# Input projection of a hybrid encoder layer: second half in reverse token order, low weight parts kept in DRAM

## The chip, the cores and the metric

The kernel runs on one core of a Trainium2 chip. The metric is the device time of one execution in microseconds (us). Three executions of the kernel before took 3480.42, 3481.12 and 3474.23 us (median 3480.42); a further one was recorded by the hardware profiler.

## The reference, cut to what matters

One encoder layer runs on two requests (256 and 2048 tokens, 2304 together, width 1024). Its input projection multiplies the normed and modulated tokens by one matrix whose 3072 columns feed two mixers:

```python
h = rmsnorm(x, norm1_g) * (1 + sc1) + sh1
proj = h @ w_in
hy = hyena_mixer(proj[..., :3 * HY_WIDTH], ...)      # 1536 columns
at = dilated_attention(proj[..., 3 * HY_WIDTH:])     # 1536 columns
mix = jnp.concatenate([rmsnorm(hy, hy_out_g), rmsnorm(at, attn_out_g)], axis=-1) @ w_out
```

Behind it come the output projection, a gated MLP and a last norm. All of it is float32.

## The kernel before, in words

**Products in three matmuls.** A float32 operand is split into a high part (a cast to the fp32r type on ACT, the Scalar engine) and a low part, the rest (a subtraction, `sub` at L203, mostly on DVE, the Vector engine). `mm3` (L208 to L210) adds high x high, weight-high x token-low and weight-low x token-high in one PSUM bank.

**Projection.** `project` works on three token passes of 768 own tokens (`PASS`, `OWN`) and, within a pass, on twelve tiles `m` of 128 columns. It is called twice: for the hyena columns (tiles 0 to 11, woven with the generation of the long filters, `filters`) and for the attention columns (tiles 12 to 23, woven with the hyena convolution and the remaining adaLN vectors, `ada_vector`). For each tile `load_w` loads 512 KB of weights (`wiraw`, L580), makes `wihi` on ACT (L583) and `wilo` on DVE (L203, called from L584), each from a pool of two buffers; then 48 matmuls per tile go to `pj`, ACT copies them out to `u` (L627, L629), and the result is transposed to token rows (`pjt`, `tt`) or stored (`d_qT`, `d_kT`). The hyena tiles also pass a short convolution (`cv`, POOL L656, DVE L659 and L662); POOL is the GpSimd engine.

**Input of a pass.** `modulated` loads eight tiles `x` (L489), multiplies them by the inverse norm (`normed`, DVE L519) and modulates them (ACT L553); `split` then makes `hThi` (ACT L571) and `hTlo` (DVE L203). The pool holds one set of the split input, so each pass's split replaces the last one's. The program names the loads of the next pass at tile `ms[5]`; the `x` tiles have eight buffers.

**Filters.** `filters` makes `F` on DVE (L439) from matmuls `fw` (L432, L433), splits it (`fhi` on ACT, `flo` on POOL), multiplies (`fs`), copies out (`fae`, ACT L420) and stores (`d_fA`, L421).

**Order.** The generators are woven by the rates in `RATES`; a scheduler of the framework then sets each engine's order of instructions, and may put one well ahead of its place in the program. SP (SyncE) issues nearly all DMAs, in one queue in order: a DMA that waits holds back those behind it.

Of the kernel before, what the change touches and what calls it, by code (L numbers as in the profile page):

```python
# [13 lines left out]
F32 = mybir.dt.float32  # L14
# [7 lines left out]
P = 128  # L22
# [167 lines left out]
class Hybrid:  # L190
# [331 lines left out]
    def first_input(self, wp, w2, psp):  # L522

        nc = self.nc
        X = []
        for i, (c0, n) in enumerate(self.PASS[0]):
            acc = w2.tile([P, 2, self.RW], F32, tag="rsacc", name="rsacc", bufs=1)[:, :, :n]
            for j in range(0, 8, 2):
                x = self.x_tile(wp, c0, n, j)
                X.append((i, j, c0, n, x))  # L530
                if j == 0:
# [5 lines left out]
            self.x_rstd(psp, acc, c0, n)  # L537
            for _, _, _, _, x in X[4 * i:]:
                self.normed(x, c0, n)
        return X  # L540

    def modulate(self, X, both=False):

        nc = self.nc
        for i, j, c0, n, x in X:
            for k in range(2):
                for r, s, e in self.segs(c0, n):
                    xs = x[:, k, s:e]
                    ga, sh = self.ga[:, 0, j + k, r:r + 1], self.mod[:, 0, j + k, r:r + 1]
                    if both and k:  # L550
                        nc.vector.tensor_scalar(out=xs, in0=xs, scalar1=ga, scalar2=sh, op0=ALU.mult, op1=ALU.add)
                    else:
                        nc.scalar.activation(xs, xs, AF.Identity, scale=ga, bias=sh)  # L553
        return X
# [19 lines left out]

    XB = 8

    def load_w(self, wp, src, k, tag, n=8, raws=3, bufs=2):
        nc = self.nc
        raw = wp.tile([P, 8, P], F32, tag="wraw", name=tag + "raw", bufs=raws)[:, :n]
        nc.sync.dma_start(out=raw, in_=src)  # L580
        hi = wp.tile([P, 8, P], F32R, tag="whi", name=tag + "hi", bufs=bufs)[:, :n]
        lo = wp.tile([P, 8, P], F32R, tag="wlo", name=tag + "lo", bufs=bufs)[:, :n]
        nc.scalar.copy(hi, raw)  # L583
        self.sub(nc.vector, lo, raw, hi)  # L584
        return hi, lo

    def project(self, hp, wp, w2, psp, ms, H=None):

        nc, a = self.nc, self.a
        pending = []  # L590

        def flush():
            while pending:
                pending.pop(0)()

        def to_tokens(src, dst, o0, o1, k):
            def go():
                for t0 in range(0, 6, 3):
                    ps = psp.tile([P, 512], F32, tag="pt", name="pjt", bufs=2)
                    for t in range(3):  # L600
                        nc.tensor.transpose(ps[:, t * P:(t + 1) * P], src[:, (t0 + t) * P:(t0 + t + 1) * P],
                                            self.ident)
                    if t0 == 0:
                        tt = wp.tile([P, 6, P], F32, tag="tt", name="tt", bufs=2)
                    nc.vector.tensor_copy(tt[:, t0:t0 + 3], ps[:, :3 * P].rearrange("p (t c) -> p t c", c=P))
                nc.sync.dma_start(out=dst[o0:o1].rearrange("(t p) c -> p t c", p=P)[:, :, k * P:(k + 1) * P], in_=tt)
            return go

        for p in range(3):
            if p == 0 and H is None:  # L610
                X = self.modulated(wp, 0)
            if p or H is None:
                H = [[], []]
                self.split(hp, X, H)
            yield
            o0, o1 = self.OWN[p]
            base = self.PASS[p][0][0]
            for m in ms:
                wh, wl = self.load_w(wp, a["w_in"][m], m, "wi", raws=2)
                u = wp.tile([P, 772], F32, tag="u", name="u", bufs=2)  # L620
                for (c0, n), hs in zip(self.PASS[p], H):
                    ps = psp.tile([P, 512], F32, tag="ps", name="pj")
                    for j in range(8):
                        self.mm3(ps[:, :n], wh[:, j], wl[:, j], hs[j][0], hs[j][1], j == 0, j == 7)
                    us = u[:, c0 - base:c0 - base + n]
                    if 12 <= m < 16:
                        nc.scalar.mul(us, ps[:, :n], -0.125)  # L627
                    else:
                        nc.scalar.copy(us, ps[:, :n])  # L629
                flush()  # L630
                src = u[:, o0 - base:o1 - base]
                if m < 12:
                    src = self.short_conv(w2, u, base, o0, o1, m)
                k = m % 4
                if 12 <= m < 20:
                    dst = self.qT if m < 16 else self.kT
                    nc.sync.dma_start(out=dst[k * P:(k + 1) * P, o0:o1], in_=src)
                else:
                    dst = self.tok[("hv", "x1", "x2", "", "", "av")[m // 4]]
                    pending.append(to_tokens(src, dst, o0, o1, k))  # L640
                yield
                if p < 2 and m == ms[2] and w2 is not None:
                    yield from self.input_rstd(wp, w2, psp, p + 1)
                if p < 2 and m == ms[5]:
                    X = self.modulated(wp, p + 1)
        flush()

    def short_conv(self, wp, u, base, o0, o1, m):
# [395 lines left out]
    def mixers(self):  # L1044
        R = self.RATES
        proj, first, atn, left, hy = (ExitStack() for _ in range(5))
        ps = self.pool(proj, "p_ps", bufs=2, space=PSUM, side="right")
        psF = self.pool(left, "f_ps", bufs=2, space=PSUM, side="left")
        hp = self.pool(proj, "p_h", side="right")
        wp = self.pool(proj, "p_w", side="right")  # L1050
        w2 = self.pool(first, "p_w2", side="right")
        self.rs = hp.tile([P, NT], F32, name="rs")
        f = self.filters(psF)
        with ExitStack() as st:
            ap = self.pool(st, "ada1", side="right")
            rows = self.ada_rows(ap)
            X = self.first_input(wp, w2, ps)
            self.weave([[self.ada_tensor(ap, psF), 8, 0], [self.ada_vector(0, ap, rows, 3, range(4, 8)), 4, 0]])
            self.ada_finish(0)
        H = [[], []]  # L1060
        for i in range(0, 8, 4):
            self.split(hp, self.modulate(X[i:i + 4], True), H)
        g = self.project(hp, wp, w2, ps, range(0, 12), H)
        for x in (g, f, f, f):
            next(x)
        self.weave([[f, R["f"], 0], [g, R["p1"], 0]])
        left.close()
        first.close()
        hb = self.pool(hy, "h_c", side="left")
        self.hyena_consts(hb)  # L1070
        wh = self.pool(hy, "h_w", side="left")
        psH = self.pool(hy, "h_ps", bufs=3, space=PSUM, side="left")

        def units():
            for r in range(2):
                yield from self.hyena(wh, psH, r)

        h = [units(), R["h1"], 0]
        with ExitStack() as st:
            ap = self.pool(st, "ada2", side="left")  # L1080

            def rest():
                rows = self.ada_rows(ap)
                for i in (2, 3, 4, 5):
                    yield from self.ada_vector(i, ap, rows, 1)
                    self.ada_finish(i)

            g = self.project(hp, wp, None, ps, range(12, 24))
            rs = rest()
            gw = [g, R["p2"], 0]  # L1090
            self.weave([h, [rs, R["ad"], 0], gw], until=rs)
        mq = ExitStack()
        self.qkp = self.pool(mq, "m_q", side="left")
        first = self.qk_tiles(self.qkp, 3)
        gw[0] = islice(g, 35 - gw[2])
        self.weave([h, gw], until=gw[0])
        gw[0] = g
        x = self.prepare(0, first)
        self.weave([h, gw, [x, 5, 0]], until=g)
        self.pre = x  # L1100
        proj.close()
        psS = self.pool(atn, "m_psS", bufs=2, space=PSUM, side="right")
        psT = self.pool(atn, "m_psT", bufs=2, space=PSUM, side="right")
        psO = self.pool(atn, "m_psO", bufs=1, space=PSUM, side="right")
        ow = ExitStack()
        self.ow = self.pool(ow, "m_r", side="right")
        h[1:] = [R["h2"], 0]
        self.weave([[self.attention(self.pool(atn, "m_a", side="right"), psS, psT, psO, first, mq), R["at"], 0], h])
        atn.close()
        return hy, mq, ow  # L1110
# [576 lines left out]
```

## Time and profile before

| | us |
|---|---|
| median of three executions | 3480.42 |
| the profiled execution | 3475.7 |
| its span, first to last instruction | 3473.9 |
| TensorE (PE) busy in the span | 3256.6 |
| DVE busy in the span | 2459.5 |

The page of the profile gives per engine the busy time and its share of the span, and cuts the span into 40 slices of 86.8 us with a busy digit in tenths. PEclk is the granted TensorE clock in tenths of full speed. In the trace the first matmul of the projection starts at 51.2 us and the last at 984.0 us; tiles 0 to 11 of the last hyena pass end shortly before 543 us, where the first attention tile's result is copied out. The first matmul of the attention itself starts at 994.8 us.

### The profile page before, as it was taken

To read this page: it belongs to the slowest core of one execution; us is meant where nothing else is said; L and a number is where in the kernel's file an instruction comes from. 1 tells how busy PE (TensorE), PEld (TensorE's weight loads), DVE (VectorE), ACT (ScalarE), POOL (GpSimd) and SP (SyncE) were. 2 spreads that over 40 slices of the span, in tenths; PEclk is the share of its full clock that TensorE was granted. 3 is DMA by queue.
4 is the path that set the end of the run, shared out by engine and by line. 5 is a ranking of instruction groups with operands and counts; after the bars stand their busy time and mean duration, and the time that the engine had idled before them with its cause. 6 is when DMAs were issued, how large, how long until landed. Compare 5 with 4: busy or idle time off the path is not lost.

```text
span 3473.9 us, 56909 instructions
## 1 busy us (share of the span) xinstructions
PE 3256.6 (94%) x20926; PEld 3001.6 (86%) x20926; DVE 2459.5 (71%) x4233; ACT 1559.7 (45%) x2895; POOL 1279.4 (37%) x1018
## 2 busy tenths in 40 slices
PE   7988899989989998998898899999999999899998
PEld 4877788778867786777898899999999999899998
DVE  7988878777576667744886766776866667457657
ACT  4576753233245645455554433334433334344443
POOL 1487661133233423210544433334533335123222
PEclk9999999999999999999899999999999999999999
DMA  6454457777585867584676523445443224557555
GB/s 246 133 163 136 149 173 234 229 255 231 192 227 176 246 189 214 173 257 137 181 214 201 186 97 123 151 163 206 148 159 143 97 90 148 181 181 239 201 192 172
DMA packets 408910, 628.02 MB, mean 181 GB/s; under 512 B 29007, under 2 KB 232015, under 8 KB 402711
## 3 DMA queue, kind: packets, MB, share of 16 engines
q1 hardware_dynamic: 355472, 593.13, 52.6%
q10 hardware_dynamic: 52072, 28.40, 2.8%
q8 instruction: 166, 2.72, 0.3%
q0 software_dynamic: 1088, 2.85, 0.2%
q14 instruction: 112, 0.92, 0.1%
HBM read 419.03 MB, written 205.25 MB: 180 GB/s over the span
## 4 chain that ended last, share of the span: by engine, by line
PE 42%; DVE 5%; DMA 2%; issue 2%; ACT 1%; POOL 1%; SPq 0%; ACTq 0%; DVEq 0%; POOLq 0%
PE w L210 9%; PE w L208 9%; PE w L209 9%; PE fd L210 5%; PE fd L209 5%; PE fd L208 5%; DVE fT L1252 1%; DMA hl<-d_opT 0%; DMA d_x1T<-ox 0%; DVE ohy L1160 0%; DVE ox L1215 0%; PE om L208 0%; POOL oat L1146 0%; PE om L209 0%; PE om L210 0%
## 5 line engine op out<-in xcount | busy, mean ns | idle before, releaser
L208 PE MATMUL w<-hh,whi 128*128 128x288 f32 (+1 forms) x2464 | 735.6, 299 | 13.2 <-ACT whi L1346 8.4
L210 PE MATMUL w<-hh,wlo 128*128 128x290 f32 (+1 forms) x2464 | 733.5, 299 | 11.2 <-POOL wlo L203 7.0
L209 PE MATMUL w<-hl,whi 128*128 128x288 f32 (+1 forms) x2464 | 735.4, 299 | 2.7 <-DVE hl L203 2.7
L208 PEld LDWEIGHTS w<-hh,whi 128*128 128x128 f32 x2464 | 471.1, 191 | 14.5 <-ACT whi L1346 8.6
L210 PEld LDWEIGHTS w<-hh,wlo 128*128 128x128 f32 x2464 | 470.4, 191 | 13.2 <-POOL wlo L203 8.0
L209 PEld LDWEIGHTS w<-hl,whi 128*128 128x128 f32 x2464 | 472.7, 192 | 3.4 <-DVE hl L203 3.2
L208 PE MATMUL pj<-hThi,wihi 128*128 128x386 f32 (+1 forms) x1152 | 402.4, 350 | 12.9 <-ACT u L629 5.4
L209 PE MATMUL pj<-hTlo,wihi 128*128 128x386 f32 (+1 forms) x1152 | 399.3, 347 | 7.1 <-DVE hTlo L203 7.1
L210 PE MATMUL pj<-hThi,wilo 128*128 128x386 f32 (+1 forms) x1152 | 401.7, 349 | 0.0
L208 PE MATMUL fd<-hh,dwh 128*128 128x288 f32 x1210 | 360.3, 298 | 12.6 <-ACT dwh L1552 12.6
L210 PE MATMUL fd<-hh,dwl 128*128 128x288 f32 x1210 | 359.0, 297 | 0.0
L209 PE MATMUL fd<-hl,dwh 128*128 128x288 f32 x1210 | 357.9, 296 | 0.0
L208 PEld LDWEIGHTS pj<-hThi,wihi 128*128 128x128 f32 x1152 | 220.2, 191 | 28.3 <-issue 7.8
L208 PEld LDWEIGHTS fd<-hh,dwh 128*128 128x128 f32 x1210 | 230.0, 190 | 13.2 <-ACT dwh L1552 12.8
L209 PEld LDWEIGHTS pj<-hTlo,wihi 128*128 128x128 f32 x1152 | 220.6, 192 | 23.9 <-issue 9.7
L210 PEld LDWEIGHTS pj<-hThi,wilo 128*128 128x128 f32 x1152 | 219.9, 191 | 11.7 <-issue 7.5
L209 PEld LDWEIGHTS fd<-hl,dwh 128*128 128x128 f32 x1210 | 229.6, 190 | 0.4
L210 PEld LDWEIGHTS fd<-hh,dwl 128*128 128x128 f32 x1210 | 228.0, 188 | 0.1
L939 PEld LDWEIGHTS aOp<-aV,aPT 128*128 128x128 f32 x1408 | 184.3, 198 | 48.8 <-issue 18.4
L735 POOL TENSOR_TENSOR ht<-ht,ht 128x512 f32<-128x512 f32 x72 | 101.7, 1413 | 338.4 <-DVE ht L734 268.2
L203 POOL TENSOR_TENSOR wlo<-ws,whi 128x512 fp32r<-128x512 f32 x88 | 131.6, 1495 | 232.3 <-ACT whi L1346 225.4
L203 POOL TENSOR_TENSOR hl<-hl,hh 128x576 fp32r<-128x576 f32 (+1 forms) x66 | 116.1, 1766 | 264.6 <-ACT hh L1494 191.4
(298 smaller groups left out, 7950.1 us busy)
## 6 DMA issues: line engine op xcount, KB each, us to landing
hl<-d_G SPq DMA_DIRECT2D x154, 288.0 KB, 5.1
dwl<-d_S SPq DMA_DIRECT2D x59, 704.0 KB, 4.9
wiraw<-in_w_in SPq DMA_DIRECT2D x72, 512.0 KB, 4.6
d_G<-cv SPq DMA_DIRECT2D x42, 576.0 KB, 2.9
wraw<-in_w_gate SPq DMA_DIRECT2D x22, 1024.0 KB, 4.8
wraw<-in_w_up SPq DMA_DIRECT2D x22, 1024.0 KB, 4.9
adat<-in_ada_t SPq DMA_DIRECT2D x36, 512.0 KB, 5.6
d_fA<-fae SPq DMA_DIRECT2D x72, 256.0 KB, 2.5
```

What stands on the lines that cost most here:

```text
L203: eng.tensor_tensor(out=lo, in0=x, in1=hi.bitcast(F32), op=ALU.subtract)
L208: mm(out, wh, xh, start=first, stop=False, skip_group_check=more)
L209: mm(out, wh, xl, start=False, stop=False, skip_group_check=more)
L210: mm(out, wl, xh, start=False, stop=last, skip_group_check=more)
L735: nc.gpsimd.tensor_tensor(out=t1, in0=t1, in1=t2, op=ALU.add)
L939: nc.tensor.matmul(po[:, i, hs], pe[:, hh, c], vt[:, x["v"] + c * x["vs"], hs], start=(c == 0), stop=(c == n - 1))
L1252: v.tensor_tensor(out=o, in0=x, in1=y, op=ALU.subtract)
```

## The change

`project` takes the order of its passes. The hyena columns keep the order 0, 1, 2. The attention columns go 2, 1, 0, and the first of these passes uses the split input that the hyena columns left (`self.H`), so that it is neither loaded, normed, modulated nor split again. In the hyena columns' first pass each `wilo` is also stored to a DRAM tensor (`d_wlo`, twelve times 512 KB, L590 of the changed kernel); in passes 1 and 2 it is loaded from there (L586) instead of being subtracted on DVE. `wihi` is made as before.

```diff
-    def load_w(self, wp, src, k, tag, n=8, raws=3, bufs=2):
+    def load_w(self, wp, src, k, tag, n=8, raws=3, bufs=2, kept=None, known=False):
...
         nc.scalar.copy(hi, raw)
-        self.sub(nc.vector, lo, raw, hi)
+        if known:
+            nc.sync.dma_start(out=lo.bitcast(F32), in_=kept)
+        else:
+            self.sub(nc.vector, lo, raw, hi)
+            if kept is not None:
+                nc.sync.dma_start(out=kept, in_=lo.bitcast(F32))
         return hi, lo
...
-        for p in range(3):
-            if p == 0 and H is None:
-                X = self.modulated(wp, 0)
-            if p or H is None:
+        lows = self.dr.tile([len(ms), P, 8, P], F32, name=f"d_wlo{ms[0]}") if w2 is not None else None
+        for p, after in zip(passes, passes[1:] + (None,)):
+            if p != passes[0]:
                 H = [[], []]
                 self.split(hp, X, H)
+            self.H = H
...
-                wh, wl = self.load_w(wp, a["w_in"][m], m, "wi", raws=2)
+                wh, wl = self.load_w(wp, a["w_in"][m], m, "wi", raws=2, kept=None if lows is None else lows[m - ms[0]],
+                                     known=lows is not None and p != passes[0])
...
-                if p < 2 and m == ms[2] and w2 is not None:
-                    yield from self.input_rstd(wp, w2, psp, p + 1)
-                if p < 2 and m == ms[5]:
-                    X = self.modulated(wp, p + 1)
+                if after is not None and m == ms[2] and w2 is not None:
+                    yield from self.input_rstd(wp, w2, psp, after)
+                if after is not None and m == ms[5]:
+                    X = self.modulated(wp, after)
...
-        g = self.project(hp, wp, w2, ps, range(0, 12), H)
+        g = self.project(hp, wp, w2, ps, range(0, 12), H, (0, 1, 2))
...
-            g = self.project(hp, wp, None, ps, range(12, 24))
+            g = self.project(hp, wp, None, ps, range(12, 24), self.H, (2, 1, 0))
```

**First place: SP's queue where hyena pass 0 ends and pass 1 begins.** `d_fA<-fae` stores a filter piece, `d_x<-tt` token rows, `x` is the next input, `wiraw` a weight tile. Before:

```order
L580 DMA wiraw<-in_w_in 128x1024
L606 DMA d_x_84<-tt 128x6x128
L421 DMA d_fA_320<-fae 128x512
L489 DMA x<-in_xT 128x2x383
L421 DMA d_fA_320<-fae 128x512
L489 DMA x<-in_xT 128x2x383 x5
L421 DMA d_fA_320<-fae 128x512
L606 DMA d_x_84<-tt 128x6x128
L489 DMA x<-in_xT 128x2x383 x2
L489 DMA x<-in_xT 128x2x386
L580 DMA wiraw<-in_w_in 128x1024
```

The same place in the changed kernel:

```order
L586 DMA wilo<-d_wlo_318 128x1024
L581 DMA wiraw<-in_w_in 128x1024
L421 DMA d_fA_321<-fae 128x512
L612 DMA d_x_84<-tt 128x6x128
L421 DMA d_fA_321<-fae 128x512
L489 DMA x<-in_xT 128x2x383 x2
L421 DMA d_fA_321<-fae 128x512
L489 DMA x<-in_xT 128x2x383 x3
L586 DMA wilo<-d_wlo_318 128x1024
L489 DMA x<-in_xT 128x2x383
L421 DMA d_fA_321<-fae 128x512
L612 DMA d_x_84<-tt 128x6x128
```

A load of `wilo` now stands ahead of nearly every load of `wiraw`, with filter stores and input loads queued behind it.

**Second place: DVE in hyena pass 2.** `F` is a filter piece, `tt` a copy of transposed rows. Before:

```order
L439 TENSOR_TENSOR F_3311<-fw_3317,fE 64x512
L439 TENSOR_TENSOR F_3312<-fw_3317,fE 64x512
L439 TENSOR_TENSOR F_3314<-fw_3324,fE 64x512
L605 COPY tt<-pjt 128x384 x2
L203 TENSOR_TENSOR wilo<-wiraw,wihi 128x1024
L439 TENSOR_TENSOR F_3313<-fw_3324,fE 64x512
L439 TENSOR_TENSOR F_3313<-fw_3406,fE 64x512
```

And now:

```order
L439 TENSOR_TENSOR F_3324<-fw_3330,fE 64x512
L439 TENSOR_TENSOR F_3325<-fw_3330,fE 64x512
L666 SCALAR_TENSOR_TENSOR cv<-u,c_short,cv 128x768
L669 SCALAR_TENSOR_TENSOR cv<-u,c_short,cv 128x767
L439 TENSOR_TENSOR F_3327<-fw_3337,fE 64x512
L439 TENSOR_TENSOR F_3326<-fw_3337,fE 64x512
```

The subtraction that stood between two filter pieces is gone, and the convolution of the tile has moved among them.

**Third place: DVE where the attention columns begin.** `hS` and `hae` belong to the hyena convolution, `adaj` to `ada_vector`. Before:

```order
L203 TENSOR_TENSOR hTlo<-x,hThi 128x772
L203 TENSOR_TENSOR hTlo<-x,hThi 128x2x384
L519 TENSOR_TENSOR x<-x,rs 128x772
L203 TENSOR_TENSOR hTlo<-x,hThi 128x2x384 x2
L687 CAST hS<-hz 64x512 x2
L694 COPY hae<-hs_5147 128x512
L203 TENSOR_TENSOR wilo<-wiraw,wihi 128x1024
L519 TENSOR_TENSOR x<-x,rs 128x772
L605 COPY tt<-pjt 128x384 x2
L203 TENSOR_TENSOR hTlo<-x,hThi 128x2x384
L519 TENSOR_TENSOR x<-x,rs 128x772
L659 SCALAR_TENSOR_TENSOR cv<-u,c_short,cv 128x768
```

And now:

```order
L611 COPY tt<-pjt 128x384 x2
L694 CAST hS<-hz 64x512 x2
L701 COPY hae<-hs_5160 128x512
L666 SCALAR_TENSOR_TENSOR cv<-u,c_short,cv 128x768
L669 SCALAR_TENSOR_TENSOR cv<-u,c_short,cv 128x767
L307 ISA adaj,mod<-adat,crows 128x1024
L307 ISA mod 128x1
L307 ISA adaj,mod<-adat,crows 128x1024
L307 ISA mod 128x1
L611 COPY tt<-pjt 128x384 x2
L203 TENSOR_TENSOR wilo<-wiraw,wihi 128x1024
```

The split of the next input (`hTlo`) and the norming of the one after it (`x<-x,rs`) no longer stand here; the norming of the next pass's input keeps its place beside hyena pass 2, and one later set of loads and normings stands at the next change of pass. From the output projection on, the order of every engine is unchanged.

## Rows read from the trace of the kernel before

**Rows 1.** The page: busy time per engine, and slices of the span.
```profile
PE 3256.6 (94%) x20926; PEld 3001.6 (86%) x20926; DVE 2459.5 (71%) x4233; ACT 1559.7 (45%) x2895; POOL 1279.4 (37%) x1018
...
PE   7988899989989998998898899999999999899998
...
DVE  7988878777576667744886766776866667457657
```

**Rows 2.** Windows: from:to, length, busy us and instructions per engine, clock, DMA share, GB/s.
```profile
core 0: us, PE busy (x) PEld busy (x) DVE busy (x) ACT busy (x) POOL busy (x), PEclk, DMA share, GB/s
205.00:510.00 305.00, 277.40 (x1417) 247.19 (x1418) 258.02 (x261) 207.37 (x362) 228.81 (x150) 0.97 0.48 148
...
570.00:985.00 415.00, 388.68 (x1915) 333.23 (x1915) 281.87 (x391) 114.91 (x183) 104.58 (x67) 0.99 0.67 217
```

**Rows 3.** PE's waits in 205 to 510: total us, times, longest.
```profile
PE fw L432 <- DVE F L439: 13.6, 10, 3.1
PE pj L209 <- DVE hTlo L203: 6.2, 4, 2.1
PE pjt L601 <- DVE cv L662: 3.7, 3, 2.6
PE fs L209 <- POOL flo L203: 3.0, 6, 1.0
```

**Rows 4.** PE's waits in 570 to 985, the two longest.
```profile
PE hs L692 <- POOL hS L203: 12.5, 15, 1.9
PE hs L778 <- DMA hD<-d_hB: 5.5, 2, 4.1
```

**Rows 5.** The `wilo` subtractions alone: all 72 (min/median/max ns), and DVE in 182 to 522, 205 to 510.
```profile
L203 DVE TENSOR_TENSOR wilo<-wiraw,wihi x72: 1201/1226/2848, 31.1 to 958.2; 128x1024 fp32r<-128x1024 f32 x72
...
182.00:522.00 340.00, 38.95 (x24) 0.97 0.51 158
205.00:510.00 305.00, 35.12 (x21) 0.97 0.48 148
```

**Rows 6.** Where the attention columns begin: PE's wait in 510 to 570, and windows.
```profile
PE pj L208 <- ACT u L627: 3.4, 1, 3.4
...
510.00:570.00 60.00, 56.58 (x313) 55.28 (x312) 52.93 (x67) 31.75 (x46) 13.82 (x8) 0.94 0.88 283
...
550.00:570.00 20.00, 16.58 (x79) 15.70 (x78) 16.59 (x23) 11.47 (x19) 0.00 (x0) 0.83 0.82 272
```

**Rows 7.** Groups of 510 to 570: busy us, mean ns | idle before.
```profile
L519 DVE TENSOR_TENSOR x<-x,rs 128x772 f32<-128x772 f32 x8 | 8.5, 1087 | 0.0
L203 DVE TENSOR_TENSOR hTlo<-x,hThi 128x772 fp32r<-128x772 f32 (+1 forms) x8 | 8.0, 1027 | 0.0
...
L553 ACT ACTIVATE x<-x,mod,ga 128x386 f32<-128x386 f32 x16 | 10.3, 701 | 8.4 <-DVE x L519 8.4
L571 ACT CAST hThi<-x 128x772 fp32r<-128x772 f32 (+1 forms) x8 | 6.6, 837 | 1.2 <-PE pj L210 1.1
```

**Rows 8.** Timeline of DVE, first and last norming of the attention columns' first loaded input.
```profile
391.05 2.06 DVE L519 TENSOR_TENSOR x<-x,rs 128x772 f32<-128x772 f32 x1
...
411.90 0.96 DVE L519 TENSOR_TENSOR x<-x,rs 128x768 f32<-128x768 f32 x1
```

**Rows 9.** DMA issues in 205 to 510, then `wiraw` in 510 to 570: KB each, us to landing.
```profile
wiraw<-in_w_in SPq DMA_DIRECT2D x21, 512.0 KB, 4.2
...
wiraw<-in_w_in SPq DMA_DIRECT2D x6, 512.0 KB, 7.4
```

**Rows 10.** Waits of SP's queue in 205 to 510: total us, times, longest.
```profile
SPq L580 <- DVE wilo L203: 50.2, 19, 6.3
SPq L464 <- DVE frn L463: 24.6, 4, 9.8
```

**Rows 11.** Timeline of SP near the end of the projection: start us, us, DMA.
```profile
899.14 1.73 SPq L867 DMA_DIRECT2D Ks<-d_kT  x3
```

**Rows 12.** DVE's longest wait in 205 to 510.
```profile
DVE F L439 <- POOL flo L203: 16.5, 12, 2.0
```

More of the change, by code (lines that the diff above doesn't have):

```diff
@@ L583, in load_w, with project @@
         nc.scalar.copy(hi, raw)
-        self.sub(nc.vector, lo, raw, hi)
+        if known:
[4 more added lines that the diff above has]
+                nc.sync.dma_start(out=kept, in_=lo.bitcast(F32))
         return hi, lo
-    def project(self, hp, wp, w2, psp, ms, H=None):
+    def project(self, hp, wp, w2, psp, ms, H, passes):
         nc, a = self.nc, self.a
```

## The prediction

> **What bounds the kernel now.** I read the page first: TensorE is busy 94% of the span, and the change leaves its matmuls as they are [rows 1]. So a gain can only come out of PE's idle time and out of stretches at a low granted clock, and the digits show where: in the first slices PE stands at 8 and 9 with DVE at 8 and 9 beside it. Next came windows by stage [rows 2]. In 205 to 510 us, hyena passes 1 and 2, PE is busy 277.40 of 305 us, so 27.6 us are idle, and the granted clock is 0.97, so about 0.03 x 305 = 9.2 us more go to stretches at the lower level (1.2 GHz). DVE is busy 258.02 us there, 84.6%. Then I asked what PE waited for in that stretch [rows 3]: DVE ended 13.6 + 6.2 + 3.7 = 23.5 us of it, mostly as filter pieces `F` that came late behind other work in DVE's queue; POOL ended 3.0. In the stage after it (570 to 985) DVE is busy 281.87 of 415 us, 67.9%, and none of PE's longest waits is for DVE; they are for POOL and DMAs [rows 4]. The reader is to see that DVE is what holds PE in the hyena passes, and hardly later.
>
> **Term 1, the subtractions of passes 1 and 2.** 24 subtractions go; they stand between 182 and 522 us and took 38.95 us, 1.62 us each, 21 of them (35.1 us) within 205 to 510 [rows 5]. They are not on PE's path themselves: they fill DVE's queue ahead of `F`, `hTlo` and `cv`. How much wait goes is estimated by a line through two stages: DVE waits cost PE 23.5 / 305 = 7.7% at 84.6% DVE load and nothing at 67.9%. Less 35.1 us, DVE would work 222.9 us in about 293, 76%; the line gives 3.7%, 10.9 us, so 12.6 us saved. The shortest of the 72 subtractions took 1.20 us and the longest 2.85 [rows 5], so part of the 1.62 is waiting, which a neighbour may inherit; at 1.20 us for 21, 25 us go, the load is 79%, the line leaves 15 us, and 8.5 are saved. I take **-11**, between the two, nearer the measured mean. Bounds: 0 (the waits stay, behind POOL) and -23.5.
>
> The Trainium skill ("SBUF — State Buffer", "Who interferes with whom") says that a DVE instruction with two SBUF inputs contends with a GpSimd instruction that reads SBUF, and that the later one blocks fully until the first ends. The spread from 1.20 to 2.85 us of one form agrees with it [rows 5]. By that rule the wait of a removed subtraction passes to the next two-input instruction, and this term would be the lower -8.5.
>
> **Term 2, the clock.** Of the 9.2 us lost at the lower level I let the same share return as of the waits, 11 / 23.5: **-4**. Bounds 0 and -9.2.
>
> **Term 3, the kept input.** One set goes: eight loads of `x`, eight normings (8.5 us of DVE), 16 modulations (10.3 us of ACT), eight casts (6.6 us of ACT) and eight subtractions (8.0 us of DVE) [rows 7]. Which place gets emptier is told by the order: an input is still normed beside hyena pass 2, as at 391 to 412 us before [rows 8] (it is now the attention columns' second pass's), so the work that vanishes is the split and the norming at 530 to 565 us. There PE waited 3.4 us for ACT's copy of `u`, and from 550 to 570 the clock was 0.83, 3.4 us lost [rows 6]. With ACT and DVE free both should go; I take **-6** of 6.8. Bounds 0 and -6.8. The DMAs have it easier too: the share was 0.88 there.
>
> **Term 4, the new loads.** A `wilo` load waits until PE ends the tile two before, because its buffer is one of two; its first use is one tile later. 24 tiles stand in 340 us, 14.2 us each. The nearest row, `wiraw` of equal size, lands after 4.2 us in this stretch and after 7.4 where the DMA share is 0.88 [rows 9]. The new loads within 205 to 510 add 21 x 0.52 MB, 36 GB/s to 148, so the share rises from 0.48 to about 0.60: 4.2 us is nearest, and some 10 us of cover are left. Behind a waiting `wilo` load stand filter stores, `wiraw` and `x` loads, but SP already stands still there: 19 times, 50.2 us in all, its `wiraw` load waited for DVE's `wilo` [rows 10], and that wait goes. Its longest wait on another DVE result is 9.8 us; such a wait ahead of a load gives 14.0 us with landing, just the cover. I take **+1** for a late load at a change of pass. Bounds: 0 and, worked out below, +36.
>
> **Edits at nothing.** The twelve stores of pass 0 wait for a subtraction that the `wiraw` load behind them waited for before, and cover by the tile's own matmuls lets them land; without that cover the next subtraction into the buffer comes one landing (4.2 us) later, still inside a tile. The reversed order makes the first quarter of q and k the last written. But k for the first heads was fetched at 899 us before [rows 11] and the first attention matmul came at 994.8, so some 95 us of projection and convolution hide it; with that gone, attention would start up to 95 us late. The new order of instructions up to the attention's end I cost at 0, unsigned: no row tells a direction.
>
> **Sum:** -11 - 4 - 6 + 1 = **-20**. The profiled execution took 3475.7 us (span 3473.9 and 1.8 around it) and would take 3455.7. It lies 4.7 us below the median of the runs, so against that median the forecast is 3480.4 - 20 = **3460.4 us**.
>
> **Rivals.** (a) *POOL becomes what holds the filters.* POOL is busy 228.81 of 305 us [rows 2], and DVE's longest wait for work is for POOL's `flo`, 16.5 us [rows 12]. If the filter chain runs at POOL's pace, DVE's free time turns into more such waits, and PE's waits for `F` stay. Only term 3 is left: 3474. For it speaks that 16.5; against it that POOL still has 25% free and that much of its busy time is shared waiting.
> (b) *The low parts come late; slower.* In place of a subtraction on a near engine stands a wait for PE's tile end, SP's queue and 512 KB of DMA. It decides once hold and landing exceed a tile's 14.2 us: 9.8 us of hold with 7.4 of landing make 17.2, 3 us too late. With half of the 24 tiles late by that, PE loses 36 us; less 20 gained, +16: 3496. Against it speaks that no row in this stretch shows `wiraw` landing above a median of 4.2, and that 9.8 us of hold came four times only.
> (c) *Full relief.* All waits for DVE and the clock losses of the stretch and of the change of pass go: -23.5 - 9.2 - 6.8 = -39.5, 3441. It needs DVE never to queue, which eight `hTlo` in a row at two changes of pass deny.
> (d) *The change does less than it says:* the kept input only moves the work, since the next pass's is normed beside hyena pass 2 as before. Then term 3 is 0 and the time is 3466. The order speaks against it: one set is gone for good.
>
> **How the numbers follow.** A measurement of this kernel can tell about 0.2%, 7 us, from no change. The forecast (gain between 8 and 32 us) gets 0.57, (d) 0.05, (c) 0.04; all three are faster: 0.66. (a) gets 0.20, read as no change. (b), and a new order that costs later stages more than the gain, get 0.14. The range goes from full relief, 3441, to a little above no change, 3482; that leaves out most of (b) and a small rest below.
>
> **What would show it.** Right: 48 `wilo` subtractions instead of 72; in the hyena passes 1 and 2 (some 15 us shorter) DVE at 75 to 79% and PE's waits for DVE at 8 to 15 us; no wait of PE for a `wilo` load over 1 us; no wait for `u` where the attention columns begin, and a clock of 1.00 there; 985 to the end as long as before within 5 us. Wrong: waits for `wilo<-d_wlo` on PE (b); DVE's wait for `flo` well above 16.5 us with `F` as late as ever (a); or a gain given back in the attention, where the order is new too.

## The result, and the profile after

Four executions of the changed kernel took 3439.68 to 3445.95 us, median **3441.85**; the ratio to the kernel before is 0.9898, 95% interval 0.9881 to 0.9915. Run again later (`e15_again`, below) it gave 0.9902, 0.9884 to 0.9919. Some 70 executions of the kernel before lay beside the experiments, with medians from 3475.1 to 3477.5; taken as 3476, the change gains 34 to 36 us. Forecast was a gain of 20: the direction holds, the range (3441 to 3482) holds by less than 1 us, the size doesn't.

The new profile's span is 3444.2 us, against 3473.9. Here is the window of the hyena passes 1 and 2 in the kernel before, from ACT's last copy of tile 11 to that of tile 35 (columns as in [rows 2]):

```profile
199.80:538.30 338.50, 308.20 (x1595) 277.16 (x1596) 287.85 (x299) 227.44 (x389) 241.18 (x158) 0.97 0.52 161
```

PE's waits in it (total us, times, longest):

```profile
PE fw L432 <- DVE F L439: 16.0, 11, 3.1
PE pj L209 <- DVE hTlo L203: 6.2, 4, 2.1
PE pjt L601 <- DVE cv L662: 4.3, 4, 2.6
PE fs L209 <- POOL flo L203: 3.0, 6, 1.0
```

The same window of the changed kernel:

```profile
202.10:516.00 313.90, 299.71 (x1595) 275.88 (x1594) 255.61 (x275) 219.14 (x374) 230.90 (x161) 0.98 0.66 211
```

And its PE's waits there:

```profile
PE fw L432 <- DVE F L439: 7.1, 5, 2.6
PE pjt L607 <- DVE cv L669: 4.3, 4, 2.1
PE pj L209 <- DVE hTlo L203: 2.3, 2, 1.5
PE fs L209 <- POOL flo L203: 0.5, 1, 0.5
```

The same 1595 matmuls take 313.9 us instead of 338.5, 24.6 less. PE's idle time (length less busy) fell from 30.3 to 14.2, its waits for DVE from 26.5 to 13.7 (16.2 in the second profile, `e15_again`). The other 8.5 us are busy time of the same matmuls: 0.01 of clock is some 4 of them, the rest is not explained. No wait for a `wilo` load is in the list. The changed kernel's tile view of `wilo` shows 48 subtractions where 72 stood [rows 5], and the 24 loads:

```profile
L203 DVE TENSOR_TENSOR wilo<-wiraw,wihi x48: 1205/1222/2278, 31.5 to 924.0; 128x1024 fp32r<-128x1024 f32 x48
L586 SPq DMA_DIRECT2D wilo<-d_wlo x24: 319/326/691, 180.3 to 496.1; - x24
```

Its waits in the same stretch, DVE's for `flo` (which answers to [rows 12]) and SP's at the new load (to [rows 10]; the 50.2 us for DVE's `wilo` are gone):

```profile
DVE F L439 <- POOL flo L203: 8.2, 8, 1.7
...
SPq L586 <- PE pjt L607: 20.2, 9, 5.2
SPq L586 <- PE pj L210: 11.1, 6, 4.7
```

At the step to the attention columns, ACT's copies of `u` mark tile 35's end and tile 36's (tile view: start of the first and last in the window). Before they stand 18.1 us apart, with the change 10.9. Before:

```profile
L627 ACT ACTIVATE u<-pj x2: 481/488/494, 543.6 to 556.4; 128x386 f32<-128x386 f32 x1, 128x384 f32<-128x384 f32 x1
L629 ACT COPY u<-pj x1: 474/474/474, 538.3 to 538.3; 128x384 f32<-128x384 f32 x1
```

With the change:

```profile
L634 ACT ACTIVATE u<-pj x2: 486/492/497, 522.0 to 526.9; 128x386 f32<-128x386 f32 x1, 128x384 f32<-128x384 f32 x1
L636 ACT COPY u<-pj x1: 471/471/471, 516.0 to 516.0; 128x384 f32<-128x384 f32 x1
```

The changed kernel's windows there; the clock is 1.00 where it was 0.83 [rows 6]:

```profile
516.00:540.00 24.00, 24.00 (x123) 20.99 (x121) 20.55 (x31) 5.42 (x10) 5.37 (x2) 1.00 0.69 232
540.00:560.00 20.00, 20.00 (x101) 17.56 (x100) 16.42 (x23) 3.60 (x6) 5.58 (x3) 1.00 0.73 251
```

By stage, from two profiles of each kernel (the second of before is the control `e14_control`), in us:

| stage | before | change | mean difference |
|---|---|---|---|
| start to tile 11 | 199.8, 199.4 | 202.1, 202.3 | +2.6 |
| tiles 12 to 35 (hyena passes 1, 2) | 338.5, 336.8 | 313.9, 318.4 | -21.5 |
| tile 36 | 18.1, 18.2 | 10.9, 10.8 | -7.3 |
| tiles 37 to 71 | 428.0, 424.1 | 422.1, 423.3 | -3.3 |
| to the first attention matmul | 10.4, 10.6 | 17.1, 17.4 | +6.8 |
| attention, up to the MLP's first `w` matmul | 918.0, 925.3 | 914.3, 914.6 | -7.2 |
| rest | 1561.1, 1561.2 | 1563.8, 1564.4 | +3.0 |

They add up to -27. The last row has a new order too, though the section on the change calls the order unchanged from the output projection on: in the traces the order of DVE differs until 1980 us before and 1951 with the change, some 70 us into that row, and ACT's nearly as long. The +3 goes with the change's order; `e10_back` below takes 1564.7 there. The two profiled executions of the change were the longest of those timed, so some 8 us of the 35 lie in executions without a profile and can't be placed.

### The profile page after: what moved, and what is told of

Its sections match the earlier page's. It is cut to its first block, busy times and chain, and to the rows that moved or that the text cites. A ratio compares the mean times of both kernels' runs of the same rounds, so it can differ in the third digit from the quotient of the medians.

```text
span 3444.2 us, 56850 instructions
## 1 busy us (share of the span) xinstructions
PE 3247.9 (94%) x20926; PEld 3006.1 (87%) x20926; DVE 2409.6 (70%) x4193; ACT 1544.0 (45%) x2871; POOL 1265.0 (37%) x1018
## 4 chain that ended last, share of the span: by engine, by line
PE 42%; DVE 5%; DMA 2%; issue 1%; ACT 1%; POOL 1%; SPq 0%; ACTq 0%; DVEq 0%; POOLq 0%
PE w L210 9%; PE w L208 9%; PE w L209 9%; PE fd L210 5%; PE fd L209 5%; PE fd L208 5%; DMA hl<-d_opT 1%; DVE hl L203 1%; DMA d_x1T<-ox 0%; DVE fT L1259 0%; PE om L208 0%; POOL oat L1153 0%; PE om L209 0%; PE om L210 0%; ACT fV L1254 0%
## 5 line engine op out<-in xcount | busy, mean ns | idle before, releaser
L209 PE MATMUL w<-hl,whi 128*128 128x290 f32 (+1 forms) x2464 | 735.1, 299 | 5.4 <-DVE hl L203 5.4
L208 PE MATMUL fd<-hh,dwh 128*128 128x288 f32 x1210 | 360.3, 298 | 12.6 <-ACT dwh L1559 12.6
L209 PEld LDWEIGHTS pj<-hTlo,wihi 128*128 128x128 f32 x1152 | 222.2, 193 | 22.3 <-issue 12.6
```

The source lines that it names most:

```text
L208: mm(out, wh, xh, start=first, stop=False, skip_group_check=more)
L209: mm(out, wh, xl, start=False, stop=False, skip_group_check=more)
```

## The experiments

Each ratio is against the kernel before on the same chip; the us are (ratio - 1) x 3476. "Passes" is the stretch from tile 11's end to tile 35's in the one profile of each.

| run | ratio (95%) | us | passes |
|---|---|---|---|
| the change | 0.9898 (0.9881 to 0.9915) | -35 | 313.9 |
| `e15_again` | 0.9902 (0.9884 to 0.9919) | -34 | 318.4 |
| `e1_lows` | 0.9940 (0.9929 to 0.9952) | -21 | 323.0 |
| `e2_input` | 0.9955 (0.9941 to 0.9969) | -16 | 341.1 |
| `e3_neither` | 0.9891 (0.9877 to 0.9904) | -38 | 313.4 |
| `e4_half` | 0.9921 (0.9907 to 0.9934) | -27 | 330.4 |
| `e5_spare` | 1.0001 (0.9992 to 1.0010) | 0 | 338.8 |
| `e6_hold` | 0.9946 (0.9935 to 0.9958) | -19 | 324.3 |
| `e7_all` | 0.9855 (0.9840 to 0.9870) | -50 | 318.7 |
| `e8_stores` | 0.9974 (0.9965 to 0.9983) | -9 | 328.6 |
| `e9_order` | 0.9956 (0.9941 to 0.9971) | -15 | 321.1 |
| `e10_back` | 0.9977 (0.9967 to 0.9987) | -8 | 338.1 |
| `e11_stores_order` | 1.0010 (1.0000 to 1.0020) | +3 | 338.8 |
| `e12_all_order` | 0.9960 (0.9945 to 0.9975) | -14 | 318.3 |
| `e13_all_back` | 0.9890 (0.9872 to 0.9908) | -38 | 316.5 |
| `e14_control` | 1.0003 (0.9991 to 1.0014) | +1 | 336.8 |

### The two parts apart

`e1_lows` gives the attention columns their own input and the order 0, 1, 2 again:

```diff
-            g = self.project(hp, wp, None, ps, range(12, 24), self.H, (2, 1, 0))
+            g = self.project(hp, wp, None, ps, range(12, 24), None, (0, 1, 2))
```

> Kept low parts alone; the attention columns take their passes as 0, 1, 2 with an input of their own. If the two parts add up, hyena passes 1 and 2 (from the end of tile 11 to the end of tile 35, 338.5 us before and 313.9 with the change) last about 314 us here too, the step to the attention columns costs what it did before (18 us from tile 35 to tile 36, where the change has 11), and the whole is about 27 us below the kernel before: near 3451. If instead the new order of instructions, and not the low parts, made the gain, the passes come back to some 330 and the whole to 3465 or more. If the reversed order is what delays the attention's start, the first attention matmul is here as much earlier as the last projection tile; if not, it gives back some 7 us here too.

`e2_input` keeps the input and stores and loads no low part:

```diff
-                wh, wl = self.load_w(..., kept=None if lows is None else lows[m - ms[0]],
-                                     known=lows is not None and p != passes[0])
+                wh, wl = self.load_w(..., kept=None, known=False)
```

> Kept input alone; all 72 subtractions stand and no low part is loaded. If the parts add up: hyena passes 1 and 2 at about 338 us as before, 7 us gained from tile 35 to tile 36, the whole 7 to 11 below before: 3467 to 3471. If the gain came from the order, or the input's part is worth nothing by itself (the next work just moves up): 3474 to 3478, or the passes become shorter here too.

The totals add up, 21 + 16 = 37 beside 35, but the input's share is twice what was expected, and the stages don't add up. With the low parts alone the passes take 323.0, not 314; with the input alone they stay as before, tile 36 gains its 6 us, and some 10 more come from later places. The attention's start comes 8 us after the last projection tile in both, 10 in the kernel before, so the 17 of the change are neither part's alone, and not the reversed order's.

### DVE's time, or SP's wait

The subtraction took DVE's time, and it also kept the raw buffer until DVE's queue had reached it, for which SP's next weight load waited. `e5_spare` brings back the time alone, `e6_hold` the hold alone, both inside the branch that loads:

```diff
+            for i in (0, 4):
+                self.sub(nc.vector, self.spare, hi[:, i:i + 4].bitcast(F32), hi[:, i:i + 4])
```

```diff
+            self.sub(nc.vector, raw[:, 0, :1], raw[:, 0, :1], hi[:, 0, :1])
```

> The change, and VectorE's time put back without what hung on it: beside each low part that is loaded stand two subtractions of 512 columns into a tile that nobody reads; SP's loads still wait for ScalarE's copy alone. Theory Q (the time in VectorE's queue made the gain): hyena passes 1 and 2 go back to 330 to 345 us and the whole to 3460 to 3475. Theory S (the gain came from SP, whose weight loads no longer wait for VectorE's low part, 52.6 us in 21 waits before): the passes stay at 314 to 318 and the whole at 3442 to 3447.

> The change, and the hold put back without the time: beside each low part that is loaded VectorE subtracts one column of the raw weights in place, so the raw buffer is again free only when VectorE's queue has come to it, but 24 full subtractions become 24 of one column. Theory Q: the gain stays, the passes at 314 to 318 us and the whole at 3442 to 3447. Theory S: SP's waits for VectorE come back (some 50 us), the passes go to 325 or more, the whole to 3455 or more.

DVE's group of the added instructions in the passes of `e5_spare` (busy us, mean ns | idle before):

```profile
L203 DVE TENSOR_TENSOR spare<-wihi 128x512 f32<-128x512 f32 x46 | 52.4, 1139 | 5.9 <-ACT wihi L584 5.0
```

The window of its passes:

```profile
201.00:539.80 338.80, 311.04 (x1604) 279.37 (x1604) 307.14 (x326) 220.94 (x376) 241.62 (x161) 0.97 0.62 199
```

In the passes the time alone gives everything back: PE waits 17.4 us for `F` again, although SP's weight loads wait for DVE only 0.9 us here. (It is 52.4 us, more than the 40.3 us of the 24 subtractions before, and the kernel has an order of its own. The whole is no measure: from the MLP's first `w` matmul on, where the edit has no instruction, it takes 1571.1 us, 7 more than the change.) The same group in `e6_hold`:

```profile
L203 DVE TENSOR_TENSOR wiraw<-wiraw,wihi 128x1 f32<-128x1 f32 x23 | 12.5, 544 | 8.0 <-ACT wihi L584 7.6
```

And its window:

```profile
201.20:525.50 324.30, 300.97 (x1596) 274.16 (x1596) 269.47 (x297) 218.73 (x375) 230.66 (x161) 0.99 0.64 204
```

The hold gives 16 of 35 us back in the whole (3455.36 us, just what theory S asked) and 6 to 10 in the passes (324.3, just short of it). The one-column instructions aren't free, 12.5 us busy and 7.6 us in which DVE stood idle for ACT's `wihi`, so about 20 us of DVE's queue came back with the hold. In the passes theory Q stands by `e5_spare`, which gave everything back without SP's wait, at a larger dose and in another order. Whether that wait adds something of its own, `e6_hold` can't tell, and the held orders below take time and wait away together.

### Do the loads cost, and is the gain a straight line

`e3_neither`, then `e4_half`:

```diff
+        if known:
+            nc.scalar.copy(hi, raw)
+            return hi, hi
...
-        if known:
-            nc.sync.dma_start(out=lo.bitcast(F32), in_=kept)
-        else:
+        if True:
             self.sub(nc.vector, lo, raw, hi)
```

```diff
-                                     known=lows is not None and p != passes[0])
+                                     known=lows is not None and p != passes[0] and m % 2 == 1)
```

> The change without its 24 loads: in hyena passes 1 and 2 the high part stands for the low part too (the third product of each weight is wrong there), so neither a subtraction nor a load is issued. If the loads cost nothing (cover enough), the passes stay within 6 us of the change's 313.9 and the whole at 3438 to 3448. If they do cost (DMA share, PE waiting for a low part, SP's queue held by PE's tile end), the passes become shorter by more than 6 us and the whole comes to 3436 or less.

> The change with only every other low part loaded in passes 1 and 2: 12 of the 24 subtractions stand. A straight line in VectorE's time puts the passes half way between the kept input alone (341) and the change (314), at 326 to 329, and the whole half way between 3460.5 and 3442, at 3451. If VectorE's waits are those of a queue that is nearly full, the first half is worth more: passes at 316 to 324, the whole at 3444 to 3448. If the gain in the passes is mostly the new order's, it is anywhere, above 330 or below 314 too.

`e3_neither` leaves out the low part (the high part stands in its place). Without the loads the passes take 313.4 us, and the whole is 3 us lower, inside the intervals: 24 loads of 512 KB cost nothing that shows. Half of the subtractions gave 27 us of the 35 in the whole, but in the passes 330.4, less than half. The two answers point to different theories, so the dose can't be read off: both kernels have an order of their own.

### What an order alone is worth

The scheduler sets a new order for every text, so every run so far mixes an edit with an order. `e8_stores` is the kernel before with the twelve stores and nothing else:

```diff
             self.sub(nc.vector, lo, raw, hi)
+            if kept is not None:
+                nc.sync.dma_start(out=kept, in_=lo.bitcast(F32))
```

> The kernel before with nothing but the twelve stores of pass 0 added: no load, no kept input, all 72 subtractions. It prices the stores and a new order of instructions that is for nothing. If the stores are free and the order is worth nothing, 3472 to 3478 and passes 1 and 2 at 336 to 341 us; the first 200 us show whether the change's 2.4 us later end of tile 11 is the stores'. If a new order alone is worth several us in a stretch, passes 1 and 2 move by 5 us or more, or the whole by 7 or more either way.

Dead stores made the kernel 9 us faster, 9 in the passes. So the next kernels hold the order: a chain of edges (issue order only, no wait for an end) ties every instruction of each of the five engines to the one ahead of it in the other kernel's order, and only the named instructions move.

```diff
+    for e, packed in ORDER.items():
...
+        row = [lists[e][int(p)] for p in places]
+        for a, b in zip(row, row[1:]):
+            tc.add_manual_dep(b, a.name, mybir.DependencyInfo(...), reason="order")
```

(`places` holds the order to be kept; the named instructions go to a list `extra`, which gets no edges.)

`e14_control` and `e11_stores_order` put this into the kernel before and `e8_stores`, `e9_order` into `e1_lows`, all three with the order of before; `e10_back` puts it into the change, with the change's order and this:

```diff
-            nc.sync.dma_start(out=lo.bitcast(F32), in_=kept)
+            self.extra.append(nc.vector.tensor_tensor(out=lo, in0=raw, in1=hi.bitcast(F32), op=ALU.subtract))
```

> The control of the held orders: the kernel before with its own order written out as ordering edges, nothing else. It should be the kernel before: 3472 to 3480 us, passes 1 and 2 at 336 to 341. If the edges themselves cost or save anything, the runs with a held order have to be read against this one.

> The twelve stores alone once more, but every other instruction held in the order of the kernel before. If the 8 us that the stores' kernel gained are the new order's: 3472 to 3479, passes 1 and 2 at 336 to 341. If the stores themselves did it (SP's or VectorE's waits moved by them): 3464 to 3470.

> Kept low parts alone, with every other instruction held, on all five engines, in exactly the order of the kernel before: 24 subtractions go, 24 loads and 12 stores come, nothing else moves. If the subtractions made the gain and the order is noise, passes 1 and 2 come to 314 to 320 us as with the change and the whole to 3448 to 3455. If the stores' kernel tells right, that some 9 us of the gain are a new order's, the relief alone is 12 to 16 us: passes at 323 to 327, the whole at 3459 to 3464. If the relief is nothing without a new order: 3472 or more.

> The change with every instruction held in exactly the change's order, but the 24 loads taken out and the 24 subtractions put back: what is left of the gain is the order's and the kept input's. If the order carries some 9 us and the input 7: 3456 to 3462, passes 1 and 2 at 325 to 331. If the subtractions are all of the gain in the passes: the passes at 336 to 342 and the whole at 3464 to 3470.

The control is the kernel before, so the edges cost nothing that shows. In the traces of all held kernels every engine's order is the one that was to be held, the named instructions aside. The stores in the old order give +3 (0 to +7) instead of -9: the 9 us were the order's. The window of the control's passes:

```profile
199.40:536.20 336.80, 309.17 (x1595) 279.02 (x1596) 286.19 (x299) 227.31 (x389) 243.99 (x158) 0.97 0.52 162
```

That of `e9_order`:

```profile
198.80:519.90 321.10, 303.01 (x1595) 275.37 (x1596) 252.66 (x276) 227.40 (x388) 227.10 (x158) 0.98 0.64 207
```

PE's two longest waits in it:

```profile
PE fw L435 <- DVE F L442: 12.6, 10, 2.9
PE pj L212 <- DVE hTlo L206: 5.1, 4, 2.1
```

DVE's wait for `flo` in it (17.7 us in the control):

```profile
DVE F L442 <- POOL flo L206: 18.0, 12, 2.0
```

And the window of `e10_back`:

```profile
201.40:539.50 338.10, 306.74 (x1595) 276.69 (x1594) 294.83 (x298) 219.82 (x374) 253.59 (x161) 0.97 0.52 161
```

DVE's wait for `flo` in it, and SP's at the weight load:

```profile
DVE F L442 <- POOL flo L206: 9.3, 10, 1.9
SPq L585 <- DVE wilo L590: 100.4, 21, 10.1
```

SP's at the same load in the control:

```profile
SPq L584 <- DVE wilo L206: 51.1, 21, 6.3
```

With the order held the relief can be read off. In the old order the passes go from 338.0 (mean of before, the control and `e11_stores_order`) to 321.1; in the change's order from 338.1 to 317.2 (mean of five profiles with that order: the change, `e15_again`, `e7_all`, `e12_all_order`, `e13_all_back`). The change's order is thus worth nothing in the passes while the subtractions stand, and about 4 us more once they are gone; that is no more than the 4.5 us between the change's two profiles, and the profiled execution of `e9_order` was the shortest of its six. In the whole, `e9_order` (3462.3) fits the forecast that left room for an order's share, with its passes 2 us shorter than that one had them; `e10_back` came with 3469.6 where the subtractions were to be all of the gain in the passes.

### All low parts kept: a kernel that beats both

`e7_all` drops the condition on `w2`, so the attention columns' low parts go through DRAM too:

```diff
-        lows = self.dr.tile([len(ms), P, 8, P], F32, name=f"d_wlo{ms[0]}") if w2 is not None else None
+        lows = self.dr.tile([len(ms), P, 8, P], F32, name=f"d_wlo{ms[0]}")
```

> The change, and the same for the attention columns: their low parts are stored in their first pass and loaded in the next two, so 24 subtractions more go. There VectorE holds PE hardly anywhere, so theory Q expects little: the stretch from tile 36 to the first attention matmul (439 us with the change) shorter by 0 to 5 us, the whole 3437 to 3443. If the loads come late there, where the DMA share is already 0.70, PE waits for a low part or for the hyena's tiles: 3446 to 3455.

It takes 3424.24 us (3418.87 to 3427.33), some 16 below the change, against both theories. Is that the relief or the order? `e12_all_order` makes the same edit in the change's order; `e13_all_back` keeps the order of `e7_all` and takes its subtractions back:

```diff
-            nc.sync.dma_start(out=lo.bitcast(F32), in_=kept)
+            if k < 12:
+                nc.sync.dma_start(out=lo.bitcast(F32), in_=kept)
+            else:
+                self.extra.append(nc.vector.tensor_tensor(out=lo, in0=raw, in1=hi.bitcast(F32), op=ALU.subtract))
```

> The low parts of the attention columns kept too, with every other instruction held in exactly the change's order: 24 subtractions go from the attention columns, 24 loads and 12 stores come. If the 18 us below the change that this edit gave are VectorE's and SP's relief: the stretch from tile 36 to the first attention matmul loses 20 us or more and the whole is 3422 to 3430. If they are a new order's: 3437 to 3443.

> The kernel that keeps the attention columns' low parts too, held in exactly its own order, but with their 24 loads taken out and the 24 subtractions put back. If its 18 us below the change are the relief: 3436 to 3446, and the stretch from tile 36 to the first attention matmul near 440 us again. If they are its order: 3420 to 3430. If an order that was made for a relief is bad without it, above 3446.

> The change once more, beside these runs: 3438 to 3446 us if the first four runs told right. Its profile shows how far two executions of one program differ by stage: passes 1 and 2 at 311 to 319 us (313.9 in the first).

`e15_again` is 3 us above its forecast, with the same ratio as the first time, and its passes are 4.5 us longer than in the first profile of the same program. The stretch from tile 35's end to the first attention matmul tells the others apart. The window of the change:

```profile
516.00:966.10 450.10, 428.75 (x2084) 367.41 (x2083) 309.96 (x436) 127.69 (x210) 113.74 (x73) 0.97 0.69 224
```

Waits in it, two of PE's and one of SP's queue:

```profile
PE hs2z L734 <- DMA hx<-d_hA: 8.0, 3, 5.1
PE hs L699 <- POOL hS L203: 4.7, 6, 2.1
...
SPq L581 <- DVE wilo L203: 38.0, 23, 6.6
```

The window of `e7_all`:

```profile
520.00:929.60 409.60, 406.06 (x2061) 357.82 (x2059) 260.96 (x386) 122.02 (x200) 101.77 (x67) 1.00 0.83 277
```

Its PE's longest wait, and SP's at the same load:

```profile
PE hs L785 <- DMA hD<-d_hB: 1.5, 1, 1.5
...
SPq L581 <- ACT wihi L584: 10.4, 13, 2.7
```

The window of `e13_all_back`:

```profile
517.60:948.40 430.80, 414.64 (x2061) 361.80 (x2059) 293.94 (x410) 122.70 (x201) 105.75 (x67) 0.98 0.72 234
```

SP's wait at that load:

```profile
SPq L585 <- DVE wilo L593: 75.0, 15, 9.1
```

DVE's group of the subtractions that were put back:

```profile
L593 DVE TENSOR_TENSOR wilo<-wiraw,wihi 128x1024 fp32r<-128x1024 f32 x24 | 31.5, 1312 | 26.6 <-ACT wihi L588 26.5
```

The window of `e12_all_order`:

```profile
518.40:980.70 462.30, 430.32 (x2084) 366.63 (x2083) 274.16 (x412) 127.64 (x210) 110.42 (x73) 0.97 0.78 258
```

PE's two longest waits in it:

```profile
PE hs2z L743 <- DMA hx<-d_hA: 12.4, 3, 5.0
PE hs L794 <- DMA hD<-d_hB: 5.8, 2, 3.2
```

In the order of `e7_all` the subtractions cost 21 us in this stretch (430.8 against 409.6), 12.6 of them PE's idle time and 8.6 the same 2061 matmuls at a lower clock, and 12 in the whole (0.9890 against 0.9855; with the two intervals taken together some 4 to 20). The 21 is the less safe: it sets the shortest of four executions of `e7_all` beside the longest of five of `e13_all_back`. That is the relief that was forecast, though the stretch is 9 us below the 440 that went with it: the order brought those. PE's list names DVE for 4.4 us only (3.9 of them `hTlo`), but SP's does: weight loads waited 75.0 us for the low part, DVE in its turn 26.5 us for ACT's `wihi`, and hyena loads stand in the same queue. That the relief came by this path was not tested apart from DVE's time. In the change's order the same edit made the stretch 12 us longer than in the change and the whole some 20 us slower, which neither forecast held: PE waits for `hx` and `hD`. The added loads stand in an SP order that was made without them; that this is the cause was only argued. The same edit is worth -16 us or +20, by the order.

## Why the prediction was right in sign and wrong in size

**Term 1 (subtractions, -11) and term 2 (clock, -4): right in size for the order that the trace showed, by the stated path in part.** In `e9_order` idle time falls by 12.2 us (30.3 to 18.1; against the control's 27.6 by 9.5) and the clock's loss by 3.7 (0.03 x 338.5 less 0.02 x 321.1); the whole is -15.3 beside the -14 of terms 1, 2 and 4. DVE's load there is 252.66 / 321.10 = 78.7%, inside the forecast 75 to 79, but PE's waits for DVE fell by 8.5 us only (26.5 to 18.0, above the forecast 8 to 15; against the control's 24.5 by 6.5). The rest of the idle time was POOL's `flo` (3.0 to 0.2) and ACT. So DVE's part was nearer the 8.5 us that the prediction worked out beside the rule of the Trainium skill ("SBUF — State Buffer", "Who interferes with whom") than the 11 it took, which doesn't prove that rule. With the change itself DVE's load is 81%, since the stretch shrank with the work, and its waits are 13.7 and, in the second profile, 16.2. The straight line through two loads would have given 20 us of waits at 81%, and gives 16 at 78.7%, where 18.0 were measured: that the change's 13.7 lies in the forecast 8 to 15 is luck.

**Term 3 (kept input, -6): right at its place**, 7.3 us at tile 36, where no wait for `u` is left and the clock is 1.00. (d) is out. In `e10_back`, the input and the change's order without relief, the whole is -8.

**Term 4 (loads, +1): right.** `e3_neither` finds no cost; the loads land in 4.0 us, 0.2 below the row it was taken from; PE never waits for one in the passes. (b) is out. So is (a) as it stood, since DVE's wait for `flo` didn't grow and `F` came earlier. But that it halved to 8.2 us with the change is the order's doing: it is 9.3 with the subtractions back in that order, and 18.0 without them in the old one. There PE's waits for `F` fell from 16.0 to 12.6 us only, so that POOL's pace may hold part of them; no run tells.

**Edits at nothing.** The stores are nearly free: in the held order the first stretch takes 199.4 us, the whole 0 to 7 more. The step that failed is the last of these: *"The new order of instructions up to the attention's end I cost at 0, unsigned: no row tells a direction."* Relief with the order held is 15 (`e9_order`), and the change's order with the input and without relief is 8 (`e10_back`), 23 in all beside the forecast 20. The 35 of the change leave 12 us, with the three intervals taken together some 3 to 20. They appear only where both meet: an order that was made for a kernel without the subtractions. Counted the other way, with the change's order held, the relief is 27 in the whole (35 less 8) and 21 in the passes, where terms 1, 2 and 4 had 14; the runs show that order and relief don't add, not which of them owns the 12. Why they don't is open; that SP's weight loads wait 100.4 us for the subtractions in the change's order and 51.1 in the old one (the control) is a hint only. About 4 of the 12 may lie in the passes, within what profiles differ; the later stages nearly cancel, so that the rest can't be placed. How large such a term can be is seen in `e8_stores` beside `e11_stores_order`: 12 us between two orders of one program. By these it should have had bounds of some 15 us to either side (an estimate); as it was, its gain side was covered by the range only because that reached to rival (c), whose mechanism did not come: 14 to 17 us of idle time are still in the passes.

**985 to the end within 5 us:** by the profiles -7.2 in the attention and +3.0 behind it, -4.2 together; but the start of the attention was 7 us later against the last projection tile than before (as in `e10_back`, 18.0 us, so with the change's order).

## What to carry to other kernels

Where a scheduler sets the order, any edit is two: the edit and a new order. Hold the order on all engines before you credit an edit, and give the order a term with bounds, here by estimate some 15 us to either side. Where orders were held, time taken from DVE was worth more than PE's waits for DVE said (some 15 us beside 8.5, 12 beside 4): look also at which queue waits for it one step further back, as SP's weight loads did for DVE. That this path makes the difference is argued here, not shown.

## What the runs showed of the hardware

**An instruction's busy time holds its blocking.** In its passes `e6_hold` has one form of 128 x 1 on DVE 23 times, from 83 to 2148 ns. Three of them in DVE's timeline (start, duration in us):

```profile
226.63 0.16 DVE L203 TENSOR_TENSOR wiraw<-wiraw,wihi 128x1 f32<-128x1 f32 x1 [1.72 <-ACT wihi L584]
284.22 1.22 DVE L203 TENSOR_TENSOR wiraw<-wiraw,wihi 128x1 f32<-128x1 f32 x1
360.37 0.54 DVE L203 TENSOR_TENSOR wiraw<-wiraw,wihi 128x1 f32<-128x1 f32 x1
```

POOL's timeline beside the last two:

```profile
283.45 1.98 POOL L203 TENSOR_TENSOR flo<-F,fhi 128x512 fp32r<-128x512 f32 x1
359.58 1.31 POOL L454 TENSOR_TENSOR acc<-acc,fabs 128x512 f32<-128x512 f32 x1
```

At 226.63 POOL was idle and it took 0.16 us. At 284.22 it ended at 285.44, POOL's at 285.43; at 360.37 at 360.91, POOL's at 360.89. Of the 23, 14 end within 0.03 us behind an instruction of POOL, and all that took over 0.2 us are among them; but three (at 206.33, 323.29 and 331.24, 0.08 to 0.17 us) ended while one of POOL's that had begun before them ran on. The Trainium skill ("SBUF — State Buffer", "Who interferes with whom") says that a DVE instruction with two SBUF inputs contends with a GpSimd instruction that reads SBUF, and the later one blocks until the first has ended; the 14 ends agree, the three don't. By that, as an estimate, part of the mean of 1.68 us of a removed subtraction (40.3 / 24) was POOL's time, and its minimum of 1.20 its own.

**A DMA share of 0.83 hardly held PE.** In `e7_all` the DMAs moved 277 GB/s over 409.6 us, and PE was idle 3.5 us of them at a clock of 1.00.
